# Feed-forward's first tiles in a hybrid decoder trunk: two casts moved behind a copy, four sums behind the low parts, ten low parts from GpSimd to VectorE

## The chip, the cores and the metric

The kernel runs on one core of one Trainium2 chip. The metric is the device time of one execution in microseconds; lower is better. The core's engines each work through a queue of their own: TensorE (PE; its weight loads are PEld), VectorE (DVE), ScalarE (ACT), GpSimd (POOL) and SyncE (SP), which here only issues transfers.

## The reference

Two layers over 1024 positions of 1024 channels, in float32. Each layer runs a retention group and a differential attention group side by side from one input projection, adds their output projection to h, and then a SwiGLU feed-forward of 2816 hidden channels:

```python
for l in range(DEPTH):
    u = rmsnorm(h, attn_norm[l])
    proj = u @ w_in[l]
    ...
    h = h + mix @ w_out[l]
    u = rmsnorm(h, ffn_norm[l])
    h = h + (jax.nn.silu(u @ w_gate[l]) * (u @ w_up[l])) @ w_down[l]
return rmsnorm(h, final_norm)
```

## The kernel before

**Products in three matmuls.** Every float32 factor is split into a high part, a cast to the matmul's rounded float32 form made by ScalarE, and a low part, the factor less its cast, made by VectorE or GpSimd. A product of two factors is then three matmuls: high by high, high by low, low by high (`product`, lines 246 to 248). A low part is line 223 for a weight (`wsplit`, the cast is line 222) and line 238 for an activation (`part`, the cast is line 237).

**Seven products for eight.** The gate and up projections of one tile (128 hidden channels) are taken as a 2 by 2 block product with seven products in place of eight. The sums of weight blocks (S1 to S4) are in `factors`: `sums` (lines 887 to 889) and `last` (line 892). The sums of activation blocks (T1 to T4) are made once in each layer, in `seven_first` and `seven_second`: line 471 the sums, line 473 casts, line 476 low parts, line 238 low parts of the others. T4' is the block that `sub(b21[i], b21[i], t2[i])` makes (four instructions of line 471); its high and low parts are the right factor of each tile's seventh product.

**The line.** `feed_forward` builds a list of products, and `Line.run` goes through it. At place n it first issues product n (12 matmuls of 128x512), then the tasks that were put down for n, in the order in which they were put down, and then product n's own followers. In this stretch ScalarE, VectorE, GpSimd and SyncE are in a manual schedule: each engine does its instructions in the order of issue, and TensorE too.

**The order at the start.** Products 0 to 11 are the first two products of tiles 0 to 5 (`NPRE` is 6), which need only the first half of the norm's results. Then come the other five of each: tile 0 has products 12, 13, 14, 15 and 18, tile 1 has 16, 17, 19, 20 and 21, tile 2 has 22 to 26, tile 3 has 27 to 31. Of a tile's five, the first adds to its bank x, the second starts its bank z, the third adds to x, the fourth to z, the fifth to x. Bank z is the same held bank of PSUM for tiles 0 to 5 (`bank_z`, line 1022). The followers of the five are in this order: the copy of x and a silu; the copy of z (`keep`, line 938, on ScalarE); `c22`, which adds x to the copy of z (line 950); `second`, which reads z (line 955); `end` (lines 960 and 961). For every second tile `end` puts down lines 998 to 1009 for the next two places.

**Where weights are split.** `split` for product n is put down at place n - 4 (`LEAD`), plus `late` for a tile's first of five. It casts on ScalarE and takes the low part on VectorE if n is in `own`, else on GpSimd. `own` is 12 to 18 for tiles 0 and 1. For tile 1 `late` is 1, so both of its first splits, for products 16 (S2) and 17 (S1), stand at place 13, whose follower is the copy of z of tile 0.

**Where the activation sums are put.** `seven_second` puts down its 46 operations when place 1 is the current one. Operations 37 to 40 are the T4' sums: two at place 10 and two at place 11. Operations 41 to 45 (room, casts and low parts of T4') are at place 14.

Of the kernel before, what the change touches and what calls it, by code (L numbers as in the profile page):

```python
# [27 lines left out]
NPRE = 6  # L28
# [118 lines left out]
class Trunk:  # L147
# [302 lines left out]
    def seven_second(self, h, gcol, b, keep, line):  # L450

        nc = self.nc
        v = nc.vector.tensor_tensor
        sl = slice(HT, T)
        parts = self.squares(h, sl, 0)
        yield 15
        y = yield from self.rsqrt_rows(parts, D, gap=9)
        own = self.t("u", 4, [P, KT, HT])
        t22, t12 = [own[:, i] for i in range(4)], [own[:, 4 + i] for i in range(4)]
        c = [slice(0, 512), slice(512, 1024)]  # L460
        b11, b21 = [keep[i // 2][:, c[i % 2]] for i in range(4)], [keep[2 + i // 2][:, c[i % 2]] for i in range(4)]
        b += [self.views(TAGS7[2]), self.views(TAGS7[3]), None, self.views(TAGS7[5]), None]
        two = [self.big("sp") for _ in range(2)]
        t2 = [two[i // 2][:, c[i % 2]] for i in range(4)]

        def norm(f, k):
            nc.vector.scalar_tensor_tensor(out=f, in0=h[k][:, sl], scalar=self.gains[:, gcol + k:gcol + k + 1],
                                           in1=y, op0=ALU.mult, op1=ALU.mult)

        def sub(out, x, z, q=None, i=0):  # L470
            v(out=out, in0=x, in1=z, op=ALU.subtract)
            if q is not None:
                nc.scalar.copy(b[q][i][0], out)

        def low(src, dst):
            v(out=dst[1], in0=src, in1=dst[0].bitcast(F32), op=ALU.subtract)
        r = range(4)
        ops = [lambda i=i: norm(t12[i], i) for i in r]
        ops += [lambda i=i: norm(t22[i], 4 + i) for i in r]
        for i in r:  # L480
            ops.append(lambda i=i: sub(b11[i], t12[i], b11[i]))
            ops.append(lambda i=i: sub(t2[i], t22[i], b11[i], 2, i))
        ops += [lambda i=i: low(t2[i], b[2][i]) for i in r]
        ops += [lambda i=i: self.part(b11[i], b[3][i], nc.vector) for i in r]

        def room(q):
            b[q] = self.views(TAGS7[q])
        ops += [lambda i=i: sub(b11[i], t22[i], t12[i]) for i in r]
        ops += [lambda i=i: self.part(t22[i], b[5][i], nc.vector) for i in r]
        ops.append(lambda: room(4))  # L490
        ops += [lambda i=i: self.part(b11[i], b[4][i], nc.vector) for i in r]
        ops += [lambda i=i: sub(b21[i], b21[i], t2[i]) for i in r]
        ops.append(lambda: room(6))
        ops += [lambda i=i: self.part(b21[i], b[6][i], nc.vector) for i in r]
        for i, op in enumerate(ops):
            line.later(line.n + (i // 3 if i < 21 else 7 + (i - 21) // 6 if i < 41 else 13), op)


    def stack(self, ps, st, sl, scale):
# [371 lines left out]
    def factors(self, line, at, pos, early=None, tags=("wr", "wr"), own=(), ahead=0, late=0):  # L871

        v = self.nc.vector.tensor_tensor
        r, s3 = {}, {}
        c = (slice(0, 512), slice(512, 1024))

        def load(i):
            r[i] = self.raw(at + i, tags[i])

        def split(n, i, k):  # L880
            src = s3[0] if i is None else r[i][:, c[k]]
            line.w[n] = self.wsplit(src, self.nc.vector if n in own else None)

        def sums():
            s3[0] = self.tmp()
            a11, a21, a22 = r[0][:, c[0]], r[1][:, c[0]], r[1][:, c[1]]
            v(out=s3[0], in0=a11, in1=a21, op=ALU.subtract)
            v(out=a21, in0=a21, in1=a22, op=ALU.add)
            v(out=a11, in0=a21, in1=a11, op=ALU.subtract)  # L889

        def last():
            v(out=r[0][:, c[1]], in0=r[0][:, c[1]], in1=r[0][:, c[0]], op=ALU.subtract)
        put = lambda n, f, *x: line.later(n - LEAD, lambda: f(*x))
        if 0 in pos:
            put(pos[0] - 2, load, 0)
            if 2 in pos:
                put(pos[2] - 3, load, 1)
            put(pos[0] - ahead, split, pos[0], 0, 0)
            if 2 in pos:
                put(pos[2] - 1, sums)  # L900
            put(pos[1] - ahead, split, pos[1], 0, 1)
            if 2 in pos:
                put(pos[2], last)
        else:
            n = pos[2] - LEAD
            n0, n1, n2 = early or (n - 4, n - 3, n - 1)
            line.later(n0, lambda: load(0))
            line.later(n1, lambda: load(1))
            line.later(n2, sums)
            line.later(n2, last)  # L910
        if 2 in pos:
            put(pos[2] + late, split, pos[2], 0, 0)
            put(pos[3], split, pos[3], 1, 0)
            put(pos[4], split, pos[4], None, 0)
            put(pos[5], split, pos[5], 0, 1)
            put(pos[6], split, pos[6], 1, 1)
# [56 lines left out]
    def feed_forward(self, l, at, h, b, norm1):  # L973
# [3 lines left out]
        line = Line()  # L977
# [11 lines left out]
        def done(t):  # L989
            def run(s):  # L990
                tiles[t] = s
                if t >= FAST:
                    nc.sync.dma_start(rest[t - FAST], s)
                elif t % 2:
                    m, s0, s1, tt, t4 = t // 2, tiles[t - 1], s, {}, {}

                    def one():
                        nc.sync.dma_start(fast[m, 1], s1)
                        tt[0] = self.big("mx")
                        v(out=tt[0][:, 0:512], in0=s0[:, 512:1024], in1=s0[:, 0:512], op=ALU.subtract)  # L1000
                        v(out=tt[0][:, 512:1024], in0=s1[:, 512:1024], in1=tt[0][:, 0:512], op=ALU.subtract)

                    def two():
                        v(out=s0[:, 512:1024], in0=s1[:, 512:1024], in1=s0[:, 512:1024], op=ALU.subtract)
                        t4[0] = self.tmp()
                        v(out=t4[0], in0=s1[:, 0:512], in1=tt[0][:, 512:1024], op=ALU.subtract)
                        nc.sync.dma_start(fast[m, 2], tt[0])
                        nc.sync.dma_start(fast[m, 0], s0)
                        nc.sync.dma_start(fast[m, 3][:, 0:512], t4[0])
                    line.later(line.n + 1, one)  # L1010
                    line.later(line.n + 2, two)
            return run
# [10 lines left out]
        first = len(line.products)  # L1023
        for t in range(HIDT):
            def room(t=t):
                st[t]["s"] = self.big("mx")
                return st[t]["s"][:, 0:512]
            kw = {"early": (-1, -1, 0), "tags": ("sp", "sp"), "own": range(2 * NPRE, 2 * NPRE + 7),
                  "places": [first + i for i in (0, 1, 2, 3, 6)]} if t == 0 else {}
            if t == 1:  # L1030
                kw = {"places": [first + i for i in (4, 5, 7, 8, 9)], "own": range(2 * NPRE, 2 * NPRE + 7),
                      "late": 1}
            self.gate_up(line, at + 2 * t, b, 2 if t < NPRE else 0, st[t], room, done(t), **kw)
        at += 2 * HIDT
        for m0 in range(0, FAST // 2, 4):
# [227 lines left out]
```

## Time and profile before

| | |
|---|---|
| median of 3 runs | 2310.18 us (2310.01 to 2485.22) |
| the profiled execution | 2310.15 us, of which the span from first to last instruction is 2308.4 us |
| mean granted TensorE clock | 0.995 |
| TensorE busy | 98% of the span |
| VectorE, ScalarE, GpSimd busy | 60%, 44%, 33% |

All times in the text are microseconds from the start of the span. In a timeline a row gives the start, the duration, the engine, the line, the operation, output and input tiles with shapes and the count; a bracket at its end gives the idle time of the engine before it and what ended it. Starts of neighbours lie closer than durations where instructions overlap.

### The profile page before, as it was taken

To read this page: it belongs to the slowest core of one execution; us is meant where nothing else is said; L and a number is where in the kernel's file an instruction comes from. 1 tells how busy PE (TensorE), PEld (TensorE's weight loads), DVE (VectorE), ACT (ScalarE), POOL (GpSimd) and SP (SyncE) were. 2 spreads that over 40 slices of the span, in tenths; PEclk is the share of its full clock that TensorE was granted. 3 is DMA by queue.
4 is the path that set the end of the run, shared out by engine and by line. 5 is a ranking of instruction groups with operands and counts; after the bars stand their busy time and mean duration, and the time that the engine had idled before them with its cause. 6 is when DMAs were issued, how large, how long until landed. Compare 5 with 4: busy or idle time off the path is not lost.

```text
span 2308.4 us, 30689 instructions
## 1 busy us (share of the span) xinstructions
PE 2263.9 (98%) x11328; PEld 1898.0 (82%) x11328; DVE 1393.8 (60%) x2576; ACT 1010.4 (44%) x1905; POOL 762.4 (33%) x608
## 2 busy tenths in 40 slices
PE   7999999999999999999999999999999999999998
PEld 5888898787788888888888888988878888888887
DVE  8777612987534333895567775059874443359856
ACT  5666533444333333543256665234443333344332
POOL 3111212122444455336121112211235444544350
PEclk9999999999999999999999999999999999999999
DMA  5212131111332322752232222112123232345422
GB/s 165 76 47 65 38 100 38 56 55 55 128 120 88 118 100 92 233 182 93 69 106 55 56 65 81 57 37 74 53 90 119 82 124 83 108 157 194 162 65 73
DMA packets 74214, 216.58 MB, mean 94 GB/s; under 512 B 8016, under 2 KB 10064, under 8 KB 74064
## 3 DMA queue, kind: packets, MB, share of 16 engines
q1 hardware_dynamic: 74064, 214.62, 28.8%
q8 instruction: 89, 1.46, 0.3%
q14 instruction: 61, 0.50, 0.1%
HBM read 162.16 MB, written 44.04 MB: 89 GB/s over the span
## 4 chain that ended last, share of the span: by engine, by line
PE 79%; DVE 11%; ACT 3%; issue 2%; DMA 2%; POOL 1%; DVEq 0%; SPq 0%; POOLq 0%; ACTq 0%
PE ps_mm L246 8%; PE ps_mm L247 7%; PE ps_mm L248 7%; PE ps_mm L271 6%; PE ps_mm L272 6%; PE ps_mm L270 6%; PE ps_s L246 4%; PE ps_s L247 4%; PE ps_s L248 4%; PE ps_t L246 3%; PE ps_t L247 3%; PE ps_t L248 3%; PE ps_mm L307 2%; PE ps_mm L305 2%; PE ps_mm L306 2%
## 5 line engine op out<-in xcount | busy, mean ns | idle before, releaser
L223 POOL TENSOR_TENSOR w<-wr,w 128x512 fp32r<-128x512 f32 x278 | 389.3, 1413 | 469.0 <-ACT w L222 433.9
L263 POOL TENSOR_TENSOR w<-wr,w 128x512 fp32r<-128x512 f32 x140 | 185.2, 1329 | 572.7 <-ACT w L262 537.6
L270 PE MATMUL ps_mm<-u,w 128*128 128x512 f32 (+1 forms) x735 | 296.0, 403 | 0.0
L271 PE MATMUL ps_mm<-u,w 128*128 128x512 f32 (+1 forms) x735 | 287.2, 391 | 2.0 <-DVE u L432 2.0
L272 PE MATMUL ps_mm<-u,w 128*128 128x512 f32 (+1 forms) x735 | 287.3, 391 | 0.0
L222 ACT CAST w<-wr 128x512 fp32r<-128x512 f32 x312 | 187.9, 619 | 142.3 <-DVE wr L889 86.5
L246 PE MATMUL ps_mm<-u,w 128*128 128x512 f32 x432 | 168.6, 390 | 0.0
L247 PE MATMUL ps_mm<-u,w 128*128 128x512 f32 x432 | 168.3, 390 | 0.0
L248 PE MATMUL ps_mm<-u,w 128*128 128x512 f32 x432 | 168.2, 389 | 0.0
L272 PEld LDWEIGHTS ps_mm<-u,w 128*128 128x128 f32 x735 | 138.0, 188 | 30.4
L271 PEld LDWEIGHTS ps_mm<-u,w 128*128 128x128 f32 x735 | 138.3, 188 | 26.1 <-DVE u L432 2.8
L270 PEld LDWEIGHTS ps_mm<-u,w 128*128 128x128 f32 x735 | 138.2, 188 | 23.9
L938 ACT COPY t<-ps_mm 128x512 f32<-128x512 f32 x76 | 44.7, 588 | 246.8 <-PE ps_mm L248 246.7
L262 ACT CAST w<-wr 128x512 fp32r<-128x512 f32 x140 | 85.7, 619 | 133.6 <-PE ps_mm L271 42.6
L305 PE MATMUL ps_mm<-w,u 128*128 128x256 f32 x448 | 128.5, 287 | 0.0
L306 PE MATMUL ps_mm<-w,u 128*128 128x256 f32 x448 | 127.7, 285 | 0.2 <-POOL w L263 0.2
L307 PE MATMUL ps_mm<-w,u 128*128 128x256 f32 x448 | 127.6, 285 | 0.0
L559 DVE CUSTOM_DVE_ANT_0 sp<-ps_s,wr 128x512 f32<-128x512 f32 (+2 forms) x192 | 103.2, 551 | 35.0 <-PE ps_s L557 33.8
L223 POOL TENSOR_TENSOR w<-t,w 128x512 fp32r<-128x512 f32 x52 | 74.9, 1440 | 146.6 <-ACT w L222 146.6
L563 ACT ACTIVATE sp<-sp,m 128x256 f32<-128x256 f32 (+7 forms) x128 | 99.1, 774 | 52.0 <-DVE m L562 51.3
L246 PE MATMUL ps_t<-u,w 128*128 128x512 f32 x288 | 114.0, 396 | 4.8 <-ACT t L938 4.8
L847 DVE TENSOR_TENSOR a<-a,ps_mm 128x512 f32<-128x512 f32 (+1 forms) x148 | 98.6, 666 | 33.1 <-PE ps_mm L248 19.5
(386 smaller groups left out, 5878.0 us busy)
## 6 DMA issues: line engine op xcount, KB each, us to landing
wr<-wts SPq DMA_DIRECT2D x190, 512.0 KB, 3.7
mx<-s_fast SPq DMA_DIRECT2D x56, 512.0 KB, 4.9
s_fast<-mx SPq DMA_DIRECT2D x48, 512.0 KB, 5.0
kb<-ka SPq DMA_DIRECT2D x64, 128.0 KB, 2.3
s_rest<-mx SPq DMA_DIRECT2D x12, 512.0 KB, 2.9
kb<-wts SPq DMA_DIRECT2D x12, 512.0 KB, 5.6
mx<-s_rest SPq DMA_DIRECT2D x12, 512.0 KB, 3.7
a<-xT SPq DMA_DIRECT2D x16, 256.0 KB, 5.4
```

What stands on the lines that cost most here:

```text
L222: nc.scalar.copy(h, src)
L223: (eng or nc.gpsimd).tensor_tensor(out=o, in0=src, in1=h.bitcast(F32), op=ALU.subtract)
L246: mm(ps, lhsT=wh[:, c], rhs=bh, start=first and i == 0, stop=False, skip_group_check=True)
L247: mm(ps, lhsT=wh[:, c], rhs=bl, start=False, stop=False, skip_group_check=True)
L248: mm(ps, lhsT=wl[:, c], rhs=bh, start=False, stop=i == 3, skip_group_check=True)
L263: nc.gpsimd.tensor_tensor(out=o, in0=raw[:, cols], in1=h.bitcast(F32), op=ALU.subtract)
L270: mm(out, lhsT=lh, rhs=rh, start=first, stop=False)
L271: mm(out, lhsT=lh, rhs=rl, start=False, stop=False)
L272: mm(out, lhsT=ll, rhs=rh, start=False, stop=last)
L305: mm(o, lhsT=uh, rhs=wh, start=k == 0, stop=False)
L306: mm(o, lhsT=uh, rhs=wl, start=False, stop=False)
L307: mm(o, lhsT=ul, rhs=wh, start=False, stop=k == KT - 1)
```

## The change

The T4' sums (operations 37 to 40) go from places 10 and 11 to place 14, directly ahead of their casts and low parts. For a tile with `late`, the first of its five splits is put off by twice `late` and the second by `late`: tile 1's splits for products 16 and 17 go from place 13 to place 14. `own` becomes 12 to 28 for tiles 0 to 3, so that the low parts of products 19 to 28 are issued on VectorE and no longer on GpSimd.

```diff
-            line.later(line.n + (i // 3 if i < 21 else 7 + (i - 21) // 6 if i < 41 else 13), op)
+            line.later(line.n + (i // 3 if i < 21 else 7 + (i - 21) // 6 if i < 37 else 13), op)
...
         if 2 in pos:
-            put(pos[2] + late, split, pos[2], 0, 0)
-            put(pos[3], split, pos[3], 1, 0)
+            put(pos[2] + 2 * late, split, pos[2], 0, 0)
+            put(pos[3] + late, split, pos[3], 1, 0)
             put(pos[4], split, pos[4], None, 0)
...
-            kw = {"early": (-1, -1, 0), "tags": ("sp", "sp"), "own": range(2 * NPRE, 2 * NPRE + 7),
-                  "places": [first + i for i in (0, 1, 2, 3, 6)]} if t == 0 else {}
+            kw = {"own": range(2 * NPRE, 2 * NPRE + 17)} if t < 4 else {}
+            if t == 0:
+                kw.update(early=(-1, -1, 0), tags=("sp", "sp"), places=[first + i for i in (0, 1, 2, 3, 6)])
             if t == 1:
-                kw = {"places": [first + i for i in (4, 5, 7, 8, 9)], "own": range(2 * NPRE, 2 * NPRE + 7),
-                      "late": 1}
+                kw.update(places=[first + i for i in (4, 5, 7, 8, 9)], late=1)
```

## Rows read from the trace of the kernel before

**Rows 1.** The profile page: the span, and the busy time of each engine with its share of the span and its instructions.

```profile
span 2308.4 us, 30689 instructions
...
PE 2263.9 (98%) x11328; PEld 1898.0 (82%) x11328; DVE 1393.8 (60%) x2576; ACT 1010.4 (44%) x1905; POOL 762.4 (33%) x608
```

**Rows 2.** Who waited for whom on TensorE over the whole span: total us, number of waits, longest.

```profile
PE ps_t L246 <- ACT t L938: 4.8, 2, 2.4
...
PE ps_mm L246 <- DVE t L950: 2.5, 2, 1.6
```

**Rows 3.** TensorE's timeline in both layers: the first matmuls of products 13, (the last of 14), 15, 16, 17, 18 and 26 in the first layer, then the first of products 15 and 26 in the second.

```profile
545.36 0.47 PE L246 MATMUL ps_t<-v,w 128*128 128x512 f32 x1 [0.55 <-ACT u L237]
...
550.99 0.39 PE L248 MATMUL ps_mm<-u,w 128*128 128x512 f32 x1
553.79 0.80 PE L246 MATMUL ps_t<-u,w 128*128 128x512 f32 x1 [2.41 <-ACT t L938]
...
558.18 0.39 PE L246 MATMUL ps_mm<-ka,w 128*128 128x512 f32 x1
...
560.90 0.39 PE L246 MATMUL ps_t<-v,w 128*128 128x512 f32 x1
...
563.62 0.40 PE L246 MATMUL ps_mm<-sp,w 128*128 128x512 f32 x1
...
587.28 0.50 PE L246 MATMUL ps_mm<-sp,w 128*128 128x512 f32 x1 [1.56 <-DVE t L950]
...
1690.48 0.80 PE L246 MATMUL ps_t<-u,w 128*128 128x512 f32 x1 [2.41 <-ACT t L938]
...
1723.31 0.51 PE L246 MATMUL ps_mm<-sp,w 128*128 128x512 f32 x1 [0.90 <-DVE t L950]
```

**Rows 4.** Windows of the first layer: busy time of PE, PEld, DVE, ACT and POOL with instructions, then the granted clock, the DMA share and GB/s.

```profile
553.50:554.00 0.50, 0.21 (x1) 0.21 (x2) 0.50 (x2) 0.50 (x2) 0.00 (x0) 0.70 0.00 0
554.00:554.50 0.50, 0.50 (x2) 0.40 (x3) 0.50 (x2) 0.50 (x2) 0.00 (x0) 0.50 0.00 0
...
557.00:557.50 0.50, 0.50 (x4) 0.41 (x3) 0.50 (x2) 0.37 (x1) 0.50 (x1) 0.89 0.00 0
...
585.00:590.00 5.00, 3.44 (x16) 2.48 (x15) 2.82 (x3) 1.14 (x2) 3.68 (x3) 1.00 0.79 288
```

**Rows 5.** ScalarE's timeline, first layer: the silu at place 12, the two casts for products 16 and 17, the copy of z, and the cast for product 29.

```profile
549.63 0.63 ACT L338 ACTIVATE kb<-kb 128x512 f32<-128x512 f32 x1
552.11 1.14 ACT L222 CAST w<-wr 128x512 fp32r<-128x512 f32 x2 [1.85 <-DVE wr L889]
553.16 0.58 ACT L938 COPY t<-ps_t 128x512 f32<-128x512 f32 x1
...
581.76 0.62 ACT L222 CAST w<-t 128x512 fp32r<-128x512 f32 x1
```

**Rows 6.** VectorE's timeline, first layer, places 9 to 15.

```profile
544.53 0.68 DVE L943 TENSOR_TENSOR acc<-ps_t,t 128x512 f32<-128x512 f32 x1
...
545.73 2.49 DVE L238 TENSOR_TENSOR u<-mx,u 128x512 fp32r<-128x512 f32 x4
...
549.95 0.68 DVE L887 TENSOR_TENSOR t<-wr,wr 128x512 f32<-128x512 f32 x1
...
552.73 1.28 DVE L471 TENSOR_TENSOR mx<-mx,sp 128x512 f32<-128x512 f32 x2
...
554.53 1.28 DVE L223 TENSOR_TENSOR w<-wr,w 128x512 fp32r<-128x512 f32 x2
555.73 0.68 DVE L223 TENSOR_TENSOR w<-sp,w 128x512 fp32r<-128x512 f32 x1
556.33 2.49 DVE L238 TENSOR_TENSOR sp<-mx,sp 128x512 fp32r<-128x512 f32 x4
558.74 0.68 DVE L950 TENSOR_TENSOR t<-ps_mm,t 128x512 f32<-128x512 f32 x1
559.34 0.68 DVE L955 TENSOR_TENSOR mx<-ps_t,t 128x512 f32<-128x512 f32 x1
```

**Rows 7.** GpSimd's timeline, first layer: the low parts for products 19 and 20, then 25 and 26, then 27 and 28.

```profile
556.99 3.00 POOL L223 TENSOR_TENSOR w<-t,w 128x512 fp32r<-128x512 f32 x1 [53.01 <-ACT w L222]
559.94 1.30 POOL L223 TENSOR_TENSOR w<-wr,w 128x512 fp32r<-128x512 f32 x1
...
573.00 2.54 POOL L223 TENSOR_TENSOR w<-wr,w 128x512 fp32r<-128x512 f32 x2
...
580.99 3.40 POOL L223 TENSOR_TENSOR w<-wr,w 128x512 fp32r<-128x512 f32 x2 [5.45 <-ACT w L222]
```

**Rows 8.** VectorE's timeline, first layer: the start of the third and the fourth tile's weight sums, and then places 22 and 23.

```profile
565.79 0.69 DVE L887 TENSOR_TENSOR t<-wr,wr 128x512 f32<-128x512 f32 x1 [5.77 <-DMA wr<-wts]
...
577.99 0.69 DVE L887 TENSOR_TENSOR t<-wr,wr 128x512 f32<-128x512 f32 x1 [1.84 <-DMA wr<-wts]
...
580.85 0.69 DVE L1000 TENSOR_TENSOR mx<-mx 128x512 f32<-128x512 f32 x1
581.57 1.67 DVE L1001 TENSOR_TENSOR mx<-mx,mx 128x512 f32<-128x512 f32 x1
583.16 1.78 DVE L1004 TENSOR_TENSOR mx<-mx,mx 128x512 f32<-128x512 f32 x1
```

**Rows 9.** The chain of work that ended last, first layer: the load of the fourth tile's second weight block, behind the low part that releases its buffer (start, us).

```profile
574.32 3.58 DMA wr<-wts
```

## The prediction

> **What bounds the kernel now.** I read the page first: TensorE is busy for 98% of the span [rows 1]. So nothing can be won except where TensorE waits, and the second view is the list of who waited for whom on TensorE over the whole span. Of its entries only two lie where the diff works: the wait on line 938 (4.8 us in two waits) and the one on line 950 (2.5 us in two) [rows 2]. The third view, TensorE's timeline, places them, once in each layer: at product 15 of the feed-forward's line, and at product 26 [rows 3]. The fourth, windows of half a microsecond, shows what the first wait costs beyond itself: the granted clock falls to 0.5 as product 15 begins and is back at 1.0 shortly after 557 us, so that product 15 lasts 553.79 to 558.18 = 4.39 us where product 16 lasts 2.72 [rows 3, 4]. That is 1.66 us lost to the clock of 1.2 in place of 2.4 GHz. After the wait before product 26 (1.56 us) the clock stayed at 1.00 [rows 3, 4]. Last come the timelines of ScalarE, VectorE and GpSimd around both places [rows 5 to 8].
>
> What the reader is to see there: product 15 adds to the bank that product 13 filled, so it needs the copy of z (line 938, issued behind product 13). On ScalarE that copy stands behind two casts of the second tile, which wait 1.85 us for VectorE's sums (line 889): casts at 552.11, copy at 553.16 [rows 5]. And VectorE has no idle time at all from 544.53 to 560.02, where line 955 ends [rows 6].
>
> **The change part by part (times of the first layer; the second is the same 1136.69 us later, 1690.48 less 553.79 [rows 3]).**
>
> *Casts behind the copy.* With twice `late` and once `late` the casts S2 and S1 go from place 13 to place 14, behind the cast of product 18. ScalarE ends the activation at 549.63 + 0.63 = 550.26 [rows 5] and then copies z by 550.9. Product 14's last matmul starts at 550.99 [rows 3], so product 15 starts some 0.23 later, at 551.22, without a wait. The cast of S2 then starts behind line 889. No DMA moves with these steps. The order in which weight buffers are taken changes (18, 16, 17 for 16, 17, 18), so that the cast for product 22 waits for product 18's end; it waits for the sums at 565.79 and later anyway [rows 8], so I cost this at nothing.
>
> *T4' sums to place 14.* Four subtractions at 0.60 each (from 552.73 to 554.53 VectorE does two of them and line 943, 1.80 for three) leave the way of the second tile's sums [rows 6]. VectorE's new order from 545.73 is: four low parts to 548.14; low part 15 to 548.74; the sums of lines 887 to 892, 2.78 (552.73 less 549.95), to 551.52; line 943 to 552.12; low parts 18, 16, 17 to 553.92; the four sums to 556.33; four low parts, 2.41 (558.74 less 556.33), to 558.74 [rows 6]. Product 16 could start at 551.22 + 2.72 = 553.94 and finds its low part ready at 553.3. That far the change does what it says.
>
> *Ten low parts from GpSimd to VectorE (products 19 to 28).* On GpSimd one costs 1.30, and 3.00 beside VectorE [rows 7]; on VectorE 0.60 [rows 6]. One of them, product 19's, now stands between line 950 and line 955.
>
> **Where the stall goes.** Products 13, 15 and 17 share one bank: `bank_z` is the same held bank for all six tiles, and product 17 begins a new sum in it. So it must wait until line 955 (place 15) has read z. Product 13 shows such a release: it starts at 545.36, 0.15 after line 943 has read that bank (544.53 + 0.68 = 545.21) [rows 3, 6]. Line 955 stands at the end of the same chain of VectorE work as before: the moved sums are all still ahead of it. Before it ended at 559.34 + 0.68 = 560.02 without a gap; now 0.60 is added: 560.62. Product 17 starts at 560.77; before, 560.90 [rows 3]. TensorE could have been there at 553.94 + 2.72 = 556.66. So of the 4.24 us that products 15 and 16 gain, 0.13 stays, and a wait of 4.1 us stands before product 17 in place of the old 2.41 before product 15.
>
> *The clock after it.* No row shows a wait of 4.1 us in this stage. Bounds: 0, as after 1.56 us [rows 4], and 1.66, as after 2.41. I take 1.66, since the new wait is longer than the one that lost the clock. Product 18 then starts at 560.77 + 2.72 + 1.66 = 565.15 (before 563.62).
>
> *Product 26.* Before, it arrived at 587.28 less 1.56 = 585.72 and waited for line 950, which came late because ahead of it VectorE's lines 1001 and 1004 took 1.67 and 1.78 beside GpSimd's low parts of products 27 and 28, against 0.69 for line 1000, of the same shape, just before [rows 7, 8]. From product 18 to 26 TensorE needs 585.72 less 563.62 = 22.10, so it arrives at 587.25. VectorE: the third tile's weight load is released by the low part of product 25, now behind line 955 of the second tile, which needs product 20's end (565.15 plus three products at 22.10/8 = 2.76: 573.4): 574.1 + 0.6 = 574.7. The load takes 3.58 [rows 9]: line 887 at 578.4 (before 577.99), sums 2.86 (580.85 less 577.99) to 581.26 [rows 8], then line 1000, line 1001 (0.72 behind it), low part 27, 1004, 1006 and low part 28 at 0.6 each: line 950 runs 585.0 to 585.7. That is 1.5 before 587.25: no wait. The load queue isn't held up earlier either: the load before it is released by the low part of product 20, on GpSimd until 561.24 [rows 7], on VectorE right behind line 955, 561.3.
>
> **Sum.** First layer: product 26 at 587.25 for 587.28, -0.03. Second layer: 1723.31 less 1136.69 = 586.62 before, 587.25 now, +0.63 [rows 3]. Together +0.6. The profiled execution took 2310.15 (span 2308.4 and 1.75 around it), the median is 2310.18. Forecast 2310.8. Behind product 27 TensorE has no wait in this stage, so what stands there is carried to the end.
>
> **The rivals.**
>
> 1. *The waits really go.* If line 955 came before product 17 asks, 4.24 in each layer would stay, and 1.56 and 0.90 at product 26: 2310.15 - 8.48 - 2.46 = 2299.2. For it: both old waits are removed at their stated cause. Against it: VectorE without a gap in [rows 6] and the one bank. Chance 0.05.
>
> 2. *The new wait keeps the clock.* Product 18 then starts at 563.49, product 26 arrives at 585.59 (VectorE's line 950, some 1.6 earlier as well, ends near 584.1), so -1.69 and -1.03: 2307.4. For it: the clock stayed after 1.56 us [rows 4]. Against: it fell after 2.41. Between them, a fall that costs half is possible. Chance 0.2.
>
> 3. *Slower: VectorE and GpSimd collide before line 950.* GpSimd still has the low parts of products 29 and 30, and ScalarE casts the first of them at 581.76 [rows 5], some 0.9 later now. Then GpSimd would run beside lines 1004, 1006 and low part 28: each 1.7 for 0.6, 3.3 in all [rows 8]. Line 950 ends at 589.0, product 26 waits 1.9 in each layer: 2310.8 + 3.8 = 2314.6, and with the clock lost again (3.3) 2317.9. For it: [rows 8]. Against: four low parts in a row at 556.33 kept 0.60 each, and it was GpSimd's that took 3.00 [rows 6, 7]; the new order there is such a row without gaps. It decides from a delay of 1.5 us on. Chance 0.12.
>
> On rival 3 the Trainium skill (SBUF — State Buffer, "Who interferes with whom") has a rule that speaks against it being mild: a VectorE operation with two SBUF inputs and a GpSimd operation that reads SBUF exclude each other, and whoever starts later waits for the whole of the other. By that rule a caught operation would wait up to a whole GpSimd operation of 1.30, so three of them 3.9 and rival 3 some 2316; by the rows 3.3 and 2314.6. Both rows agree with it in kind: either side can be the one that waits.
>
> **Chances.** Forecast as worked out 0.55, rival 1 0.05, rival 2 0.2, rival 3 0.12; 0.08 for what I don't see. The likeliest one's own range is 2309.5 to 2312. The range to hold the time 8 times in 10 takes in rival 2, with some room, and rival 3 without a second fall of the clock: 2306.5 to 2314.6. Against a bound of 2%, about what a measurement of this kernel can tell from no change (46 us), every case is "within": even rival 1 is 0.5%. So 0.98, and 0.01 on either side.
>
> **What would show it.** Right: no wait of product 15 on line 938; the copy of z at about 550.3; a wait of some 4 us of TensorE before the matmuls of product 17, put down to VectorE's line 955, in both layers; a granted clock of 0.5 for some three microseconds behind it; no wait on line 950; ten low parts of line 223 fewer on GpSimd in each layer. Wrong: product 17 starting well before 560.6 (then VectorE's chain was shorter than counted), no fall of the clock, lines 1004 and 1006 at 1.7.

## The result, and the profile after

The changed kernel takes 2313.36 us (median of 22 runs, 2312.20 to 2315.24), the kernel before 2309.98 (22 runs beside it). The ratio is 1.0016, with a 95% interval of 1.0010 to 1.0021: some 3.4 us slower, inside the range of the prediction and in the direction of its sum, but with 3.4 where the sum had 0.6. It lies above the 2309.5 to 2312 that the prediction gave its likeliest case; the range holds it because it takes in rival 3. One of the 22 runs before, at 2485.22, was in a slower state and is not in the ratio. The profiled execution's span is 2311.6 (before 2308.4).

The page: GpSimd has 20 instructions fewer and VectorE 20 more than in [rows 1], the ten low parts of each layer.

```profile
span 2311.6 us, 30647 instructions
...
PE 2264.3 (98%) x11328; PEld 1898.2 (82%) x11328; DVE 1406.6 (61%) x2596; ACT 1010.5 (44%) x1905; POOL 731.8 (32%) x588
```

Who waited for whom on TensorE, whole span (total us, number, longest): line 938 of [rows 2] is gone, and line 955 stands first, with 7.9 us where that had 4.8. Line 950 is still there.

```profile
PE ps_t L246 <- DVE mx L955: 7.9, 2, 3.9
...
PE ps_mm L246 <- DVE t L950: 2.0, 2, 1.0
```

TensorE's timeline, first matmuls of products 12, 15, 16, 17, 18, 26 and 27 of the first layer, then 17, 18 and 26 of the second, to be read beside [rows 3]:

```profile
541.68 0.39 PE L246 MATMUL ps_mm<-ka,w 128*128 128x512 f32 x1
...
550.96 0.39 PE L246 MATMUL ps_t<-u,w 128*128 128x512 f32 x1
...
553.68 0.39 PE L246 MATMUL ps_mm<-ka,w 128*128 128x512 f32 x1
...
560.50 0.47 PE L246 MATMUL ps_t<-v,w 128*128 128x512 f32 x1 [3.94 <-DVE mx L955]
...
564.91 0.40 PE L246 MATMUL ps_mm<-sp,w 128*128 128x512 f32 x1
...
587.99 0.50 PE L246 MATMUL ps_mm<-sp,w 128*128 128x512 f32 x1 [0.98 <-DVE t L950]
...
590.87 0.40 PE L246 MATMUL ps_o<-ka,w 128*128 128x512 f32 x1
...
1697.62 0.64 PE L246 MATMUL ps_t<-v,w 128*128 128x512 f32 x1 [3.95 <-DVE mx L955]
...
1702.02 0.40 PE L246 MATMUL ps_mm<-sp,w 128*128 128x512 f32 x1
...
1725.15 0.50 PE L246 MATMUL ps_mm<-sp,w 128*128 128x512 f32 x1 [1.03 <-DVE t L950]
```

The reader sees products 15 and 16 follow each other without a wait, and then 3.94 us of nothing before product 17. Product 17 to 18 lasts 4.41 (564.91 less 560.50) in place of 2.72: the clock fell again, to 0.66 on average over the window from 560 to 565. Windows of the first layer (the window's length, then busy time of PE, PEld, DVE, ACT, POOL, then granted clock, DMA share, GB/s), beside [rows 4]:

```profile
555.00:560.00 5.00, 1.56 (x7) 0.95 (x6) 5.00 (x9) 2.85 (x6) 0.00 (x0) 1.00 0.00 2
560.00:565.00 5.00, 4.50 (x13) 3.59 (x14) 1.65 (x3) 2.14 (x4) 0.00 (x0) 0.66 0.48 131
565.00:570.00 5.00, 5.00 (x24) 4.05 (x23) 4.71 (x8) 2.25 (x4) 0.00 (x0) 1.00 0.24 84
```

ScalarE's timeline, against [rows 5]: the copy of z now comes right behind the activation, ahead of the two casts.

```profile
549.90 0.57 ACT L938 COPY t<-ps_t 128x512 f32<-128x512 f32 x1
550.37 0.62 ACT L222 CAST w<-sp 128x512 fp32r<-128x512 f32 x1
550.89 1.14 ACT L222 CAST w<-wr 128x512 fp32r<-128x512 f32 x2
```

VectorE's timeline, against [rows 6 and 8], and GpSimd's, against [rows 7]:

```profile
553.66 2.49 DVE L471 TENSOR_TENSOR mx<-mx,sp 128x512 f32<-128x512 f32 x4
556.07 2.49 DVE L238 TENSOR_TENSOR sp<-mx,sp 128x512 fp32r<-128x512 f32 x4
558.48 0.68 DVE L950 TENSOR_TENSOR t<-ps_mm,t 128x512 f32<-128x512 f32 x1
559.08 0.68 DVE L223 TENSOR_TENSOR w<-t,w 128x512 fp32r<-128x512 f32 x1
559.68 0.68 DVE L955 TENSOR_TENSOR mx<-ps_t,t 128x512 f32<-128x512 f32 x1
...
578.53 0.69 DVE L887 TENSOR_TENSOR t<-wr,wr 128x512 f32<-128x512 f32 x1 [0.49 <-DMA wr<-wts]
...
583.25 0.68 DVE L1004 TENSOR_TENSOR mx<-mx,mx 128x512 f32<-128x512 f32 x1
583.85 1.78 DVE L1006 TENSOR_TENSOR t<-mx,mx 128x512 f32<-128x512 f32 x1
585.55 1.78 DVE L223 TENSOR_TENSOR w<-wr,w 128x512 fp32r<-128x512 f32 x1
587.26 0.68 DVE L950 TENSOR_TENSOR t<-ps_mm,t 128x512 f32<-128x512 f32 x1
```

```profile
583.36 1.71 POOL L223 TENSOR_TENSOR w<-t,w 128x512 fp32r<-128x512 f32 x1 [79.64 <-ACT w L222]
585.04 1.74 POOL L223 TENSOR_TENSOR w<-wr,w 128x512 fp32r<-128x512 f32 x1
```

VectorE is without a gap up to line 955 (560.36), with the T4' sums, their low parts and product 19's low part still ahead of it. Later, line 1006 and the low part of product 28 take 1.78 each beside GpSimd's low parts of products 29 and 30.

### The profile page after: what moved, and what is told of

It is laid out like the page before. It is cut to its first block, busy times and chain, and to the rows that moved or that the text cites. A ratio compares the mean times of both kernels' runs of the same rounds, so it can differ in the third digit from the quotient of the medians.

```text
span 2311.6 us, 30647 instructions
## 1 busy us (share of the span) xinstructions
PE 2264.3 (98%) x11328; PEld 1898.2 (82%) x11328; DVE 1406.6 (61%) x2596; ACT 1010.5 (44%) x1905; POOL 731.8 (32%) x588
## 4 chain that ended last, share of the span: by engine, by line
PE 79%; DVE 12%; ACT 3%; DMA 2%; issue 2%; POOL 1%; DVEq 0%; SPq 0%; ACTq 0%; POOLq 0%
PE ps_mm L246 7%; PE ps_mm L247 7%; PE ps_mm L248 7%; PE ps_mm L271 6%; PE ps_mm L272 6%; PE ps_mm L270 6%; PE ps_s L246 4%; PE ps_s L248 4%; PE ps_s L247 4%; PE ps_t L246 3%; PE ps_t L248 3%; PE ps_t L247 3%; PE ps_mm L307 2%; PE ps_mm L305 2%; PE ps_mm L306 2%
## 5 line engine op out<-in xcount | busy, mean ns | idle before, releaser
L223 POOL TENSOR_TENSOR w<-wr,w 128x512 fp32r<-128x512 f32 x262 | 367.5, 1416 | 449.5 <-ACT w L222 422.7
L263 POOL TENSOR_TENSOR w<-wr,w 128x512 fp32r<-128x512 f32 x140 | 184.8, 1326 | 572.5 <-ACT w L262 553.5
L223 POOL TENSOR_TENSOR w<-t,w 128x512 fp32r<-128x512 f32 x48 | 66.1, 1378 | 198.4 <-ACT w L222 198.4
```

Of the source, the lines that this page charges most:

```text
L223: (eng or nc.gpsimd).tensor_tensor(out=o, in0=src, in1=h.bitcast(F32), op=ALU.subtract)
L263: nc.gpsimd.tensor_tensor(out=o, in0=raw[:, cols], in1=h.bitcast(F32), op=ALU.subtract)
```

## The experiments

Theory A is that of the prediction: the wait moves from product 15 to product 17, because line 955, which must read bank z before product 17 may start, stands at the end of the same VectorE chain as before. Theory B: the ten low parts moved to VectorE are what costs. C and D are stated where they are tried. A table of all runs stands at the end of this section; distances are starts in TensorE's timeline, less that of product 12.

**The casts alone.** Only the two `put` lines of the diff, on the kernel before.

> The kernel before with the two casts alone moved to place 14. Distances are from the start of product 12, first layer; before: product 15 at 11.86, 17 at 18.97, 18 at 21.69, 27 at 48.24. Theory A (the wait moves on to line 955, the reader of bank z, which stands at the end of VectorE's chain): product 15 at about 9.3 without a wait; product 16 waits some 1.4 for its low part; product 17 waits about 2 for line 955 and starts at about 18.2, since VectorE's chain is as long as before; product 27 between 47.0 and 48.6, and the time within 2 us of before. Theory B (what costs is the low parts moved to VectorE, the casts are a gain by themselves): product 17 starts near 14.7 to 16 and the time is 4 us or more below before.

Measured 2314.54 us, ratio to before 1.0018 (1.0009 to 1.0027): neither theory had this. Product 15 is at 9.31 and product 16 waits 1.3 for its low part, as A had it; but product 17 starts at 20.41, not at 18.2. The timelines of TensorE (inside product 16), VectorE and GpSimd say why:

```profile
555.48 0.50 PE L248 MATMUL ps_mm<-ka,w 128*128 128x512 f32 x1 [1.30 <-DVE w L223]
```

```profile
555.95 4.65 DVE L238 TENSOR_TENSOR sp<-mx,sp 128x512 fp32r<-128x512 f32 x4
560.53 0.68 DVE L950 TENSOR_TENSOR t<-ps_mm,t 128x512 f32<-128x512 f32 x1
561.13 0.67 DVE L955 TENSOR_TENSOR mx<-ps_t,t 128x512 f32<-128x512 f32 x1
```

```profile
555.60 1.57 POOL L223 TENSOR_TENSOR w<-t,w 128x512 fp32r<-128x512 f32 x1 [52.01 <-ACT w L222]
557.13 1.72 POOL L223 TENSOR_TENSOR w<-wr,w 128x512 fp32r<-128x512 f32 x1
```

With the casts put off, GpSimd gets its two low parts (products 19 and 20) 1.0 us earlier, counted from product 12 (14.06 for 15.06), just before VectorE's four low parts rather than in their middle, and these take 4.65 in place of 2.49 [rows 6]. The 2.2 us go straight into product 17. So the casts are no gain by themselves, and the low parts of products 19 and 20 on VectorE belong with them.

**The T4' sums alone.** `i < 37` for `i < 41`, on the kernel before.

> The kernel before with the T4' sums alone moved to place 14. Theory A: the casts for 16 and 17 come 1.2 earlier, product 15 starts at about 10.7 from product 12 (before 11.86), product 17 again waits for line 955, about 2 us, and starts at about 18.2; the time within 2 us of before. Theory B: product 17 follows product 15 without a wait, at about 16.2, and the time is 3 us or more below before.

Measured 2309.93, ratio 1.0002 (0.9993 to 1.0011). Product 15 at 10.65, product 17 after a wait of 1.72 for line 955 at 18.14: A's numbers. The clock stayed at 1.00 after this wait (product 17 to 18 lasts 2.87), which A had left open.

**The low parts alone.** The `own` lines of the diff, on the kernel before.

> The kernel before with the ten low parts alone moved to VectorE. Theory A: the wait on line 938 before product 15 stays at 2.4 and product 17 starts at 19.0 as before, because line 955 0.6 later still comes in time; the wait before product 26 goes from 1.56 and 0.90 to at most 0.9, so product 27 is at 46.7 to 47.6 (before 48.24 in the first layer, 47.56 in the second) and the time is 0 to 2.5 us below before. Theory B: the low parts themselves cost: product 17 later than 19.5 or product 26 waiting over 1.6, the time 2 us or more above before.

Measured 2309.41, ratio 0.9997 (0.9989 to 1.0006). The wait before product 15 is 2.41 as before, product 17 at 19.03, the wait before product 26 0.89 and 1.0; product 27 at 47.64 and 47.80, a little above A's span. The load of the ten low parts on VectorE is thus not what costs; B falls.

**Another bank for tile 1's z.** On the changed kernel:

```diff
-            st[t]["bank_z"] = lambda tag: hold("t")
+            st[t]["bank_z"] = lambda tag, t=t: hold("s" if t == 1 else "t")
```

> The changed kernel, with tile 1's bank z put into the other held bank (tag s, last read by line 943 at place 11) in place of the one that tile 0's z has. Nothing is taken from VectorE's chain. Theory A: the wait before product 17 (3.9 us) goes, product 17 starts at about 14.7 from product 12 (18.8 in the changed kernel), the clock doesn't fall, product 18 is at 17.5 (23.2); VectorE's line 950 then sets product 26, which waits 1.5 to 4; product 27 at 44 to 47 (49.2), so 4 to 10 us off the changed kernel's time in both layers together. Rival D (VectorE's chain holds product 17 by something else than the bank, such as its weight's low part or the copies): product 17 stays near 18.8 and the time within 1.5 us of the changed kernel's.

Measured 2308.78, ratio to before 0.9995 (0.9986 to 1.0004), 4.6 us below the changed kernel. The wait before product 17 is gone (14.73) with VectorE's work unchanged (line 955 starts 18.0 after product 12 in both kernels), so it was the bank's reader and nothing else; D falls. The wait that I expected before product 26 came already before product 21, which adds to the bank that line 950 must read first (2.83, in the second layer 2.72), and it cost the clock once more; product 27 of the first layer, at 47.13, is just past the expected 47. TensorE's timeline (products 17, 21 and 22; the last two 4.37 apart) and windows:

```profile
558.14 0.39 PE L246 MATMUL ps_s<-v,w 128*128 128x512 f32 x1
...
572.37 0.51 PE L246 MATMUL ps_mm<-sp,w 128*128 128x512 f32 x1 [2.83 <-DVE t L950]
...
576.74 0.48 PE L246 MATMUL ps_mm<-ka,w 128*128 128x512 f32 x1
```

```profile
570.00:575.00 5.00, 2.63 (x8) 2.09 (x9) 4.12 (x7) 1.89 (x4) 0.00 (x0) 0.85 0.01 2
575.00:580.00 5.00, 5.00 (x19) 4.03 (x18) 2.99 (x5) 0.22 (x1) 0.00 (x0) 0.81 0.54 179
```

**T4' behind line 955.** On the changed kernel, the T4' sums, casts and low parts go to place 16:

```diff
-            line.later(line.n + (i // 3 if i < 21 else 7 + (i - 21) // 6 if i < 37 else 13), op)
+            line.later(line.n + (i // 3 if i < 21 else 7 + (i - 21) // 6 if i < 37 else 15), op)
```

> The changed kernel with the T4' sums, their casts and low parts at place 16, behind lines 950 and 955, in place of 14. VectorE's eight operations (4.8 us) leave the way to line 955. Theory A: line 955 ends some 4.8 earlier, product 17 starts without a wait at about 14.7 from product 12 (18.8 in the changed kernel), product 18 waits at most 0.5 for the low parts, the clock stays, the fourth tile's load is released earlier and product 26 doesn't wait; product 27 at 41.5 to 43 (49.2), so some 12 to 15 us off the changed kernel's time: about 2299 to 2302. Rival D: a wait of like size comes back before product 18 or 26, and the time is within 3 us of the changed kernel's.

Measured 2303.10, ratio to before 0.9970 (0.9958 to 0.9981), 10.3 below the changed kernel. Products 17 and 18 follow at 14.74 and 17.46 without any wait: VectorE's timeline has line 955 ahead of the eight operations now.

```profile
556.08 0.68 DVE L955 TENSOR_TENSOR mx<-ps_t,t 128x512 f32<-128x512 f32 x1
556.68 0.68 DVE L223 TENSOR_TENSOR w<-wr,w 128x512 fp32r<-128x512 f32 x1
557.28 2.49 DVE L471 TENSOR_TENSOR mx<-mx,sp 128x512 f32<-128x512 f32 x4
...
579.91 1.79 DVE L1006 TENSOR_TENSOR t<-mx,mx 128x512 f32<-128x512 f32 x1
581.62 1.78 DVE L223 TENSOR_TENSOR w<-wr,w 128x512 fp32r<-128x512 f32 x1
```

It misses the expected 2299 to 2302 by a little: product 26 waits 0.92 and 1.2, behind line 1006 and low part 28 at 1.78 to 1.79 again (in the second layer lines 1004 and 1006), and product 21 waits 0.4. Product 27 comes at 44.05 and 44.19, where A had 41.5 to 43.

**Low parts 29 to 31 on VectorE too.** On the changed kernel, `own` to `2 * NPRE + 20`.

> The changed kernel with the low parts of products 29, 30 and 31 on VectorE too. It tells the collision with GpSimd apart from VectorE's load: Theory A: lines 1006 and the low part of product 28 go from 1.78 to 0.69, line 950 comes 2 us earlier, the wait before product 26 (1.0) goes in both layers, and the time is 1 to 2.5 us below the changed kernel's. Theory B (VectorE has too much to do): the wait stays or grows and the time is the same or above.

Measured 2311.79, ratio to before 1.0007 (0.9998 to 1.0015), 1.6 below the changed kernel. The intervals of the two overlap, so the reading rests on the trace. VectorE's timeline:

```profile
583.77 0.68 DVE L1006 TENSOR_TENSOR t<-mx,mx 128x512 f32<-128x512 f32 x1
584.37 0.68 DVE L223 TENSOR_TENSOR w<-wr,w 128x512 fp32r<-128x512 f32 x1
584.98 0.68 DVE L950 TENSOR_TENSOR t<-ps_mm,t 128x512 f32<-128x512 f32 x1
```

Line 1006 and low part 28 take 0.68 each, line 950 starts at 584.98 (587.26), and the wait before product 26 is gone in both layers, with three low parts more on VectorE. So it was the collision, not the load. In the second layer this profile lost more to the clock (product 17 to 18 lasts 5.25), so product 27 is at 47.83 in the first layer and at 49.17 in the second.

**Filling the wait.** On the changed kernel, ahead of tile 1's second product:

```diff
+                if "fill" in st and q == 3:
+                    for _ in range(17):
+                        nc.tensor.matmul(st["fill"]("s"), lhsT=self.ones, rhs=b[0][0][0], start=True, stop=True)
                 yield from self.product(st[name], line.w.pop(n), b[q], bool(tag))
...
+            if t == 1:
+                st[t]["fill"] = hold
```

> The changed kernel with 17 matmuls more (128x512, into a bank whose contents nobody reads any more) ahead of product 17 in each layer, in the time in which TensorE waits. It takes the price of the clock by itself. Theory A: product 17 still starts near 18.8 from product 12 (17 x 0.227 = 3.9), the granted clock stays at 1.0, product 18 is at 21.6 in place of 23.2; product 26 then waits up to 1.6 more for line 950 or arrives earlier, product 27 at 47.6 to 49.0 (49.2); the time 0.5 to 3.3 us below the changed kernel's. Theory C (the clock's fall is the whole of the 3.4 us that the change cost): the time is at that of before or below, 3.3 us under the changed kernel.

Measured 2311.20, ratio to before 1.0005 (0.9996 to 1.0014), 2.2 below the changed kernel. TensorE's timeline has the 17 matmuls where it waited, and the windows a full clock:

```profile
556.39 4.12 PE L934 MATMUL ps_s<-u,c_ones 128*128 128x512 f32 x17
```

```profile
560.00:565.00 5.00, 5.00 (x23) 3.82 (x22) 2.01 (x4) 2.73 (x5) 0.00 (x0) 1.00 0.47 126
```

Product 17 is at 18.84 as without them, product 18 at 21.68 and 21.66 in place of 23.23: 1.55 to 1.57 us a layer is the price of the clock. Product 27 comes at 47.31 and 47.63, in the first layer 0.3 earlier than A had it. The two theories don't exclude each other: A says where the wait stands, C what it costs against before. That the clock is the whole of the 3.4 us, as C has it, isn't shown: 2.2 came back, and before lies inside the interval.

In the changed kernel VectorE's chain sets product 17 (18.8). Before, line 955 ended 18.09 after product 12 and would have let it start near 18.2; TensorE, which had lost 1.66 to the clock in product 15, came at 18.97. So all but some 0.7 of that loss lay inside what product 17 would have had to wait anyway, and in the changed kernel the loss lies behind product 17, in the open. Without it the change costs about nothing at this place (product 18 at 21.68, before 21.69).

**T4' at place 16 and low parts 29 to 31 on VectorE.** The edits of the fifth and the sixth experiment together.

> The changed kernel with the T4' sums and their low parts at place 16, and the low parts of products 29 to 31 on VectorE too. Theory A: product 17 and 18 without a wait as with place 16 alone (14.7 and 17.5 from product 12), lines 1006 and low part 28 at 0.69, the wait before product 26 (0.9 to 1.2) goes; product 27 at 42.9 to 43.3 (44.1 with place 16 alone); the time about 2301, 9 us below before. Theory B (VectorE has too much): a wait comes back before product 28 to 31 and the time is not below 2303.

Measured 2301.76, ratio to before 0.9958 (0.9944 to 0.9971): the lowest median, 11.6 below the changed kernel's. Its interval overlaps that of T4' at place 16 alone; in the trace product 27 comes 1.1 and 1.4 earlier than there, at 42.92 and 42.82, and line 1006 and low part 28 are without a collision:

```profile
579.48 0.69 DVE L1006 TENSOR_TENSOR t<-mx,mx 128x512 f32<-128x512 f32 x1
580.08 0.68 DVE L223 TENSOR_TENSOR w<-wr,w 128x512 fp32r<-128x512 f32 x1
580.69 0.68 DVE L950 TENSOR_TENSOR t<-ps_mm,t 128x512 f32<-128x512 f32 x1
```

**T4' at place 16 with the low parts on GpSimd.** The casts and `i < 37 else 15` on the kernel before, `own` as before.

> The two casts at place 14 and the T4' sums and low parts at place 16, but the low parts of products 19 to 28 on GpSimd as in the kernel before. Theory A: GpSimd's low parts of products 19 and 20 now run beside VectorE's low parts 16 and 17 or lines 950 and 955 and beside the T4' sums, so those are caught as with the casts alone; product 17 starts at 14.7 to 16, product 18 waits 1 to 3 for T4', lines 1001 to 1006 take 1.7 again; product 27 at 44.5 to 47.5; the time 2303 to 2308. Theory B (moving low parts to VectorE is needless load): product 27 at 43.5 or earlier and the time at or below that with place 16 alone, 2303.

Measured 2305.10, ratio 0.9976 (0.9968 to 0.9985). Product 18 does not wait (17.46), where A had 1 to 3: GpSimd's low parts of products 19 and 20 run beside lines 950 and 955, and only one VectorE low part is caught. Then VectorE's lines 1001 (1.68) and 1004 stand beside GpSimd's low parts 27 and 28, and line 1006 beside the next:

```profile
580.09 1.78 DVE L1004 TENSOR_TENSOR mx<-mx,mx 128x512 f32<-128x512 f32 x1
581.79 1.76 DVE L1006 TENSOR_TENSOR t<-mx,mx 128x512 f32<-128x512 f32 x1
```

```profile
577.90 3.41 POOL L223 TENSOR_TENSOR w<-wr,w 128x512 fp32r<-128x512 f32 x2 [5.43 <-ACT w L222]
```

The wait before product 26 is 1.97 and 1.9; behind the first the clock fell (product 26 to 27 lasts 4.44), behind the second it stayed (2.89). With T4' out of the way, the low parts on VectorE as far as product 28 are worth 2 us at most, and this isn't clear of noise: 2305.10 against 2303.10, where the kernel before took 2311.18 and 2310.28 beside them, and the intervals overlap. With 29 to 31 it is 3.3 (2301.76, the same kernel before beside both), and the intervals barely overlap.

The changed kernel and the one before in the table are those of the 22 runs; beside the first four experiments the kernel before took 2309.98 as well, beside the second group (from T4' at place 16 to the filled wait) 2310.28, beside the last two 2311.18.

| kernel | median us | product 15 (first layer) | 17 | 18 | 26 | 27 (first, second layer) |
|---|---|---|---|---|---|---|
| before | 2309.98 | 11.86 | 18.97 | 21.69 | 45.35 | 48.24, 47.56 |
| changed | 2313.36 | 9.28 | 18.82 | 23.23 | 46.31 | 49.19, 49.24 |
| casts alone | 2314.54 | 9.31 | 20.41 | 24.83 | 46.79 | 49.58, 50.54 |
| T4' sums alone | 2309.93 | 10.65 | 18.14 | 21.01 | 44.39 | 47.28, 47.46 |
| low parts alone | 2309.41 | 11.87 | 19.03 | 21.75 | 44.74 | 47.64, 47.80 |
| other bank for z | 2308.78 | 9.29 | 14.73 | 17.64 | 44.34 | 47.13, 46.75 |
| T4' at place 16 | 2303.10 | 9.30 | 14.74 | 17.46 | 41.17 | 44.05, 44.19 |
| low parts to 31 | 2311.79 | 9.32 | 18.85 | 23.11 | 45.04 | 47.83, 49.17 |
| wait filled | 2311.20 | 9.33 | 18.84 | 21.68 | 44.42 | 47.31, 47.63 |
| T4' at 16, low parts to 31 | 2301.76 | 9.30 | 14.74 | 17.46 | 40.12 | 42.92, 42.82 |
| T4' at 16, low parts as before | 2305.10 | 9.30 | 14.74 | 17.46 | 41.55 | 45.99, 44.40 |

## Why the prediction was right, and where its sum was short

**Product 15.** Right: foreseen at 551.22, that is 9.29 from product 12 (541.93 before), measured 9.28.

**Where the stall goes.** Right, and to the tenth: product 17 foreseen at 560.77, 18.84 from product 12, measured 18.82 and 18.83, after a wait of 3.94 and 3.95 for line 955. The other bank and T4' at place 16 each take this wait away alone, from the two sides of the cause: the bank, and the chain in front of its reader. One reading under it is weaker than it was put: the row of product 13 names a cast of ScalarE (line 237) as what ended its wait, so it does not show that the bank was released 0.15 after its reader. Product 17 does: it starts at 560.50, 0.14 after line 955 has ended.

**The clock after it.** Right: product 18 foreseen 23.22 from product 12, measured 23.23 in both layers. Rival 2 did not happen. Filled with matmuls, the same wait keeps the clock. That the size came out so well is in part luck: behind a wait of 3.94 the second layer of another run (low parts to 31) lost 2.53, more than the upper bound of 1.66.

**Product 26.** Here the sum fell short. The step put line 1000, line 1001, low part 27, lines 1004 and 1006 and low part 28 at 0.6 to 0.7 each, and so line 950 43.1 after product 12 and 1.5 ahead of TensorE. It came at 45.6 (587.26 less 541.68): two of the six took 1.78. (The fourth tile's sums themselves were on time: line 887 foreseen 36.5 after product 12, measured 36.9.) That is rival 3 with two operations caught in place of three, 2.2 us in place of 3.3, and product 26 waited 0.98 and 1.03 where 1.9 was its price. The argument against it, that a row of operations without a gap keeps GpSimd out, was read from [rows 6, 7] and is wrong as a rule: line 1006 followed line 1004 without a gap and was caught, and with the casts alone four low parts in a row lost 2.2 together. [rows 8] held the counterexample: there line 1004 began at 583.16, before line 1001 had ended (581.57 and 1.67), and took 1.78. In [rows 7] GpSimd's operation began in the middle of the row and was the one that waited; with the casts alone it began just before. Taking away GpSimd's part (low parts to 31) removed the whole wait.

**The sum.** From product 12 to 27 the changed kernel needs 0.95 more in the first layer (49.19 for 48.24) and 1.68 in the second: 2.63, where the prediction had 0.6. The collision's wait of 0.98 and 1.03 is the difference. The rest of the 3.2 between the two spans lies outside the places that the diff touches, and the sum had it at nothing: ahead of product 12 of the first layer and between the two stretches the changed kernel is 0.8 shorter, and behind product 27 of the second layer 1.4 longer. There TensorE waits 1.1 for weight casts around 2086 and 2099, a place where other profiles here show 0 to 0.9 in one or the other layer. Whether the change moves it or it varies by itself was not tried.

On the rule for rival 3 of the Trainium skill (SBUF — State Buffer, "Who interferes with whom"): the rows agree that VectorE's and GpSimd's operations hold each other up, and that the later one waits for the end of the other. GpSimd's operation at 583.36 began 0.11 behind line 1004 and lost 0.4 (1.71 for 1.30); line 1006 began 0.49 behind that and ended 0.56 after its end (585.63 for 585.07), and so lost 1.1 (1.78 for 0.68). What is lost is thus the rest of the other operation, and 1.1 is the price to use here, not the 1.30 that the prediction named as the most.

## What to carry to other kernels

When a wait is taken from one engine's queue, look for the next reader that the same buffer or bank has, and count the queue in front of that reader: here two waits two products apart hung on the same VectorE chain, and taking work out of the chain ahead of that reader (2303.10) gained what moving casts could not. A wait that only moves is not neutral where the clock falls behind it: what counts is whether the slow stretch lies ahead of the next thing to wait for, or behind it. And work that is set free earlier on one engine can land beside another engine's critical row: the casts alone cost 4.6 us, though they did what they were to do at product 15.

## What the runs showed that I had not expected

The granted clock stayed at 1.00 after waits of 1.56 and 1.72 and fell after waits of 2.41, 2.83 and 3.94 us; with the low parts on GpSimd and T4' at place 16 it fell after 1.97 in one layer and stayed after 1.9 in the other. After like waits before product 17 the loss differed: product 17 to 18 lasted 4.26 and 5.25 in the two layers of one profile (low parts to 31) and 4.42 and 5.25 in those of another (casts alone), where 2.72 is the undisturbed length.

Four VectorE low parts in a row took 2.49 when GpSimd's operation began in their middle, and 4.65 when it had begun 0.35 earlier than they. What decides it for a row that is already running, as for line 1006 behind line 1004, is open.
